# A hybrid decoder block on one core: one bank per token tile in the mixers, four weight slots in whole fp32, and one-hots on ScalarE

## The chip, the core and the metric

The kernel runs on one core of a Trainium2 chip. The metric is the device time of one execution in microseconds (us), and the median of several executions is what two kernels are compared by. The engines are called as the profile calls them: PE (TensorE matmul), PEld (its weight loads), DVE (VectorE), ACT (ScalarE), POOL (GpSimd) and SP (SyncE, which here only issues transfers).

## The reference, cut to what matters

512 tokens of width 1024 pass one layer: two token mixers beside each other, then a retrieval feed-forward in which every token picks 128 of 16,384 experts.

```python
h = rms_norm(x, norm1_g)
proj = h @ w_in
hq, hf, hi, hog, aq, ak, av, ga, gb = split(proj)
y_a = hgrn2_mixer(hq, hf, hi, hog, lb, hg_norm_g)          # gated recurrence, 4 heads
y_b = dilated_attention_mixer(aq, ak, av, q_norm_g, k_norm_g)
merged = sigmoid(ga) * (y_a @ w_branch_a) + sigmoid(gb) * (y_b @ w_branch_b)
x = x + merged @ w_out
h2 = rms_norm(x, norm2_g)
# PEER: 8 heads, top 16 of 128 keys twice, top 16 of the pairs: 128 experts a token
hid = einsum('thkd,td->thk', u[idx], h2)
a = gelu(hid) * gate
x = x + einsum('thk,thkd->td', a, v[idx])
```

All is float32. The kernel keeps that precision on PE in one of two ways: a whole fp32 product, which the profile shows as two records per matmul, or a split one, in which each operand is the sum of a high and a low half in fp32r and three products (high by high, high by low, low by high) are added.

## The kernel before, in words

Tokens come in four tiles of 128. The work has four stages, and I cut the trace by them.

- **First front**, 0 to 158 us: `Front((0,), split=False)` takes tile 0 through both mixers, the output product and the query product. Its products are whole fp32.
- **Second front**, 158 to 640 us: `Front((1, 2, 3), split=True)` does the same for the other three tiles with split products. `slot` loads weights, 256 columns of a matrix at a time (a slot), in units of four blocks of 128 rows (512 KB, two buffers `w`); `halves` makes `wh` on ACT (L98) and `wl` on DVE, or every fifth one on POOL (L99). `proj_T` puts 256 output columns on the partitions and streams 384 tokens; `proj_N` puts tokens on the partitions. `proj_N` kept two token tiles in one PSUM bank of the three called `pp`, and `products` held the second tile back until the slot's other products were done. Under this stage run `routing(0)` (top-16 searches on DVE, L536 to L615) and `u_steps(0)`: for tile 0 each expert's row of `u` is gathered by an indirect transfer of POOL (L638) and multiplied and summed with the token on DVE (L650), 128 rows.
- **Middle**, 640 to 1058 us: 72 blocks of `hidden` (tiles 1 and 2 against all experts, whole fp32, `ph<-h,ub`); `routing` of tiles 3, 1 and 2; and `scatter_steps`, 24 groups of 16 tokens, which turn gates and indices into a dense table. A group takes four one-hot pairs: `e1` (L689) and `e2` (L692) on DVE, `eg` which is `e2` times the weight, on ACT for `k` in `ACTW = (4, 12)` (L696) and on DVE otherwise (L698), then four matmuls into `pg` (L703, eight records), and ACT's copy to `Gx` (L704). `Gx` goes to DRAM as `g_d` (L706). Meanwhile 44 rows of `u` for tile 3 are gathered and summed (`u_steps(3)`, 0.6 of a row a block). A gather is tied to the `gelu` of the block just issued, which is `behind[0]`; its sum follows it in the program.
- **Final**, 1058 to 1781 us: 128 blocks of `acc` (split products with `v`, 18 matmuls), 56 more blocks of `hidden` with split products, the other rows of `u`, and 128 rows of `v` for tile 3. `Gc` is a group of eight blocks of the dense table, read back from `g_d` (L851, 1.5 MB), in two buffers by turns; DVE multiplies it by `pre` (L855) before `ah` and `al` are made of it.

Each engine runs its instructions in one fixed order, found when the kernel is built by a scheduler that estimates times; so the place of an instruction in its queue can differ from the place in the code.

Of the kernel before, what the change touches and what calls it, by code (L numbers as in the profile page):

```python
# [56 lines left out]
ACTW = (4, 12)  # L57
# [16 lines left out]
def kernel(ctx: ExitStack, tc: tile.TileContext, x, wst, par, cst, cols, g2, keys, u, v, ut, vr, out):  # L74
# [72 lines left out]
    class Front:  # L147


        def __init__(self, tiles, split, after_unit):  # L150
# [6 lines left out]
            lT = hp.tile([P, KC, NM], F32R, name="xl")[:, :, :N] if split else None  # L157
            g1 = par_sb[:, C_G1:C_G1 + KC]
            xs = hp.tile([P, NM // P, D], F32, name="pairB")
            for t in range(n):  # L160
# [5 lines left out]
                for c in range(0, KC, 4):  # L166
# [19 lines left out]
        def slot(self, i, ks):  # L186

            src = lambda k, n: wst[i][:, k * 256:(k + n) * 256].rearrange("p (k c) -> p k c", k=n)
            for k0 in range(ks.start, ks.stop, UK):
                n = min(UK, ks.stop - k0)  # L190
                if not self.split and k0 % (2 * UK):
# [7 lines left out]
                if not self.split:  # L199
                    yield k0 - ks.start, [w[:, k] for k in range(n)]  # L200
                    continue
# [6 lines left out]
        def products(self, i, ks, x, outs, w_stays):  # L208


            last = ks.stop - ks.start - 1
            units = []
            for k0, ws in self.slot(i, ks):
                units.append((k0, ws))
                for out, cut, alone in outs:
                    if alone:
                        accumulate(out, ws, x, cut, w_stays, k0, last)
            for out, cut, alone in outs:
                for k0, ws in units if not alone else ():
                    accumulate(out, ws, x, cut, w_stays, k0, last)  # L220

        def proj_T(self, i, x=None, ks=slice(0, KC)):

            outs = [psb.tile([P, 512], F32, name="pp")[:, :self.N] for _ in range(2)]
            self.products(i, ks, self.hT if x is None else x, [(pt, slice(j * P, (j + 1) * P), True) for j, pt in enumerate(outs)], True)
            return enumerate(outs)

        def proj_N(self, i, x=None):

            outs, parts = [], []  # L230
            for t0 in range(0, self.n, 2):
                m = min(2, self.n - t0)
                pt = psb.tile([P, 2, 256], F32, name="pp")[:, :m]
                parts += [(pt[:, t], slice((t0 + t) * P, (t0 + t + 1) * P), t == 0) for t in range(m)]
                outs.append((slice(t0, t0 + m), pt))
# [3 lines left out]
        def proj_hgrn(self):  # L239
# [4 lines left out]
            vs = hp.tile([P, 2, NM // P, 512], F32, name="vs")  # L244
            self.vt, self.sil = vs[:, 0], vs[:, 1]
# [26 lines left out]
            self.qd, self.ki, self.ksT = sq, G2, lf  # L272
            for b in range(2):
# [66 lines left out]
        def proj_attn(self):  # L340
# [3 lines left out]
            for b in range(3):  # L344
# [3 lines left out]
                for t in range(n if b else 0):  # L348
                    k0 = (T0 + t) * RQ
                    for r in range(NR):  # L350
                        nc.scalar.dma_start(out=vres[k0:k0 + RQ, b - 1, r], in_=vt[r::NR, t])
            for b in range(3):
# [3 lines left out]
                for ts, pt in self.proj_N(W_IN + 11 + b):  # L356
# [6 lines left out]
                for j in range(2):  # L363
                    pk2 = ps.tile([P, NM // P, P], F32, name="pt")
                    for t in range(n):
                        nc.tensor.transpose(pk2[:, t], kn[:, t, 2 * j:2 * j + 2].rearrange("p n e -> p (n e)"), ident)
                    nc.scalar.activation(kT[:, 2 * b + j, self.t0:self.t0 + N], pk2[:, :n].rearrange("p t q -> p (t q)"),
                                         AF.Copy, scale=kgain)
# [571 lines left out]
```

## Time and profile before

| | us |
|---|---|
| median of 3 executions (lowest, highest) | 1778.53 (1771.76, 1779.42) |
| the profiled execution, its own time | 1782.34 |
| its span, first to last instruction | 1780.6 |
| PE busy, DVE busy, ACT busy over the span | 1637.9, 1343.1, 702.0 |

How to read it: a busy PE is not PE at its best, since the ends of pipelined matmuls are modelled; the distance from one start to the next is the better price. The profile's share of time by engine is an average over four stages with different limits, so stretches are read one by one: in each, which wait of PE ends last, and which engine ended it. "granted clock" is the share of TensorE's full clock in a stretch.

### The profile page before, as it was taken

How to read it: one execution, taken by the hardware profiler on the slowest of the kernel's cores; microseconds unless marked ns; L12 is line 12 of the kernel's file. 1: busy time of each engine (PE TensorE's matmuls, PEld its weight loads, DVE VectorE, ACT ScalarE, POOL GpSimd, SP SyncE). 2: the span in 40 equal slices, each digit the busy share in tenths (PEclk: the TensorE clock that was granted, in tenths of full speed). 3: DMA queues.
4: the chain of work that ended last, by engine and by line, in shares of the span. 5: the costliest groups of instructions: out<-in, count | busy, mean ns of one | idle time of the engine just before them, and what ended most of it. 6: DMA issues, size and time to landing. Idle time of an engine off the chain costs nothing.

```text
span 1780.6 us, 26815 instructions
## 1 busy us (share of the span) xinstructions
PE 1637.9 (92%) x9725; PEld 1449.5 (81%) x9725; DVE 1343.1 (75%) x2805; ACT 702.0 (39%) x1283; POOL 663.1 (37%) x502
## 2 busy tenths in 40 slices
PE   8998969789978799899999979999999999999997
PEld 7887969679867798787888967788888878887886
DVE  3112999888888649997996567778788878888787
ACT  3323443324334544432454563333334333333332
POOL 0000256676552004344342114343344454454442
PEclk9999979989998899999999989999999999999999
DMA  8776368779885326565657769899999889998988
GB/s 289 233 231 229 105 229 280 261 250 327 304 313 203 126 100 217 207 210 189 232 200 247 246 214 332 314 327 333 342 344 337 305 308 340 342 326 318 332 296 297
DMA packets 173812, 473.41 MB, mean 266 GB/s; under 512 B 14832, under 2 KB 62192, under 8 KB 173680
## 3 DMA queue, kind: packets, MB, share of 16 engines
q1 hardware_dynamic: 116272, 268.47, 44.3%
q0 software_dynamic: 55296, 201.35, 31.9%
q10 hardware_dynamic: 2112, 1.88, 0.3%
q8 instruction: 77, 1.26, 0.3%
q14 instruction: 55, 0.45, 0.1%
HBM read 442.80 MB, written 27.79 MB: 264 GB/s over the span
## 4 chain that ended last, share of the span: by engine, by line
PE 39%; DVE 29%; DMA 23%; issue 5%; ACT 2%; POOL 2%; DVEq 0%; SPq 0%; POOLq 0%; ACTq 0%
PE pp L112 15%; PE acc L866 13%; DMA Gc<-g_d 7%; PE ph L112 7%; DMA w<-in_wst_dram 4%; DMA row<-in_u_dram,idx 2%; DVE e L689 2%; DVE h2g L669 2%; DVE rowx L650 2%; DMA rowx<-in_v_dram,idx 2%; DMA vb<-in_vr_dram 2%; DVE rq L650 2%; PE pg L703 1%; DVE wl L99 1%; DVE eg L698 1%
## 5 line engine op out<-in xcount | busy, mean ns | idle before, releaser
L112 PE MATMUL ph<-h,ub 128*128 128x256 f32 x1152 | 266.2, 387 | 0.0
L866 PE MATMUL acc<-vl,ah 128*128 128x512 f32 x768 | 241.2, 395 | 10.4 <-DVE vl L862 10.3
L112 PEld LDWEIGHTS ph<-h,ub 128*128 128x128 f32 x1152 | 219.3, 195 | 30.2 <-ACT eg L696 0.2
L866 PE MATMUL acc<-vh,al 128*128 128x512 f32 x768 | 239.9, 394 | 0.0
L866 PE MATMUL acc<-vh,ah 128*128 128x512 f32 x768 | 221.5, 392 | 3.6 <-ACT vh L860 3.6
L638 POOL DMA_INDIRECT rowx<-in_v_dram,idx x96 | 154.4, 1608 | 153.1 <-DVE h2g L669 62.4
L638 POOL DMA_INDIRECT rowx<-in_u_dram,idx x96 | 120.1, 1251 | 222.5 <-DVE rowx L650 65.4
L98 ACT ACTIVATE ah<-Gc 128x384 fp32r<-128x384 f32 x128 | 67.0, 524 | 318.9 <-PE acc L866 310.7
L866 PEld LDWEIGHTS acc<-vl,ah 128*128 128x128 f32 x768 | 143.2, 190 | 43.9 <-DVE vl L862 14.7
L866 PEld LDWEIGHTS acc<-vh,al 128*128 128x128 f32 x768 | 145.6, 190 | 31.7
L866 PEld LDWEIGHTS acc<-vh,ah 128*128 128x128 f32 x768 | 139.9, 188 | 29.7 <-ACT vh L860 4.0
L862 DVE TENSOR_TENSOR vl<-vb,vh 128x1024 fp32r<-128x1024 f32 x128 | 156.2, 1220 | 10.2 <-ACT vh L860 10.0
L860 ACT ACTIVATE vh<-vb 128x1024 fp32r<-128x1024 f32 x128 | 135.9, 1062 | 53.9 <-DMA vb<-in_vr_dram 50.9
L638 POOL DMA_INDIRECT rq<-in_u_dram,idx x96 | 119.8, 1248 | 92.1 <-DVE rq L650 57.6
L650 DVE SCALAR_TENSOR_TENSOR rowx<-rowx,h2g 128x1024 f32<-128x1024 f32 x96 | 121.2, 1267 | 33.2 <-DMA rowx<-in_u_dram,idx 33.0
L650 DVE SCALAR_TENSOR_TENSOR rq<-rq,h2g 128x1024 f32<-128x1024 f32 x96 | 132.5, 1383 | 16.3 <-DMA rq<-in_u_dram,idx 15.3
L98 ACT ACTIVATE wh<-w 128x512 fp32r<-128x512 f32 x144 | 88.7, 628 | 130.1 <-PE pp L112 65.1
L669 DVE SCALAR_TENSOR_TENSOR h2g<-rowx,hid,h2g 128x1024 f32<-128x1024 f32 x95 | 121.6, 1280 | 19.8 <-DMA rowx<-in_v_dram,idx 19.7
L112 PE MATMUL ph<-hH,ul 128*128 128x256 f32 x448 | 126.4, 282 | 5.4 <-DVE ul L99 5.4
L112 PE MATMUL ph<-hH,uh 128*128 128x256 f32 x448 | 126.0, 281 | 3.8 <-ACT pre L814 3.8
L703 PE MATMUL pg<-eg,e 128*128 128x128 f32 x768 | 105.3, 291 | 22.7 <-DVE eg L698 15.7
L112 PE MATMUL ph<-hL,uh 128*128 128x256 f32 x448 | 126.1, 281 | 0.0
(289 smaller groups left out, 3624.1 us busy)
## 6 DMA issues: line engine op xcount, KB each, us to landing
ub<-in_ut_dram SPq DMA_DIRECT2D x128, 512.0 KB
vb<-in_vr_dram SPq DMA_DIRECT2D x128, 512.0 KB
w<-in_wst_dram SPq DMA_DIRECT2D x107, 512.0 KB
g_d<-Gx SPq DMA_DIRECT2D x24, 960.0 KB
Gc<-g_d SPq DMA_DIRECT2D x15, 1536.0 KB
wh<-in_wst_dram SPq DMA_DIRECT2D x37, 256.0 KB
wl<-in_wst_dram SPq DMA_DIRECT2D x33, 256.0 KB
pairB<-in_x_dram SPq DMA_DIRECT2D x5, 512.0 KB
```

The source lines that it names most:

```text
L98: nc.scalar.activation(hi, x, AF.Copy)
L99: (eng or nc.vector).tensor_tensor(out=lo, in0=x, in1=hi.bitcast(F32), op=ALU.subtract)
L112: nc.tensor.matmul(out, l, r, start=(k == 0 and i == 0), stop=(k == last and i == len(ops) - 1))
L638: d = nc.gpsimd.indirect_dma_start(out=r, out_offset=None, in_=src, in_offset=bass.IndirectOffsetOnAxis(ap=index, axis=0))
L650: nc.vector.scalar_tensor_tensor(r, r, 1.0, h2g[T], op0=ALU.mult, op1=ALU.mult, accum_out=hid[:, g, j:j + 1])
L669: nc.vector.scalar_tensor_tensor(acc, r, hid[:, g, j:j + 1], acc, op0=ALU.mult, op1=ALU.add)
L689: nc.vector.tensor_tensor(out=e1, in0=iota[:, None, :, 0].to_broadcast(by_token), in1=pk[:, ti, 0, tk, None].to_broadcast(by_token), op=AL ...
L698: nc.vector.tensor_tensor(out=eg, in0=e2.rearrange("p k q -> p q k"), in1=pkw[:, ti, tk, None].to_broadcast(by_token), op=ALU.mult)
L703: nc.tensor.matmul(pt[:, q], e1[:, q0 + q], eg[:, q0 + q], start=True, stop=True)
L860: behind[:] = [nc.scalar.activation(vH, vb, AF.Copy)]
L862: nc.vector.tensor_tensor(out=vL, in0=vb, in1=vH.bitcast(F32), op=ALU.subtract)
L866: nc.tensor.matmul(acc[t][c], l.rearrange("p g t -> p (g t)")[:, t * P:(t + 1) * P], r[:, c * 512:(c + 1) * 512], start=(b == 0 and i == 0 ...
```

## The change

Seven edits.

1. In the second front the normalised input is also kept whole (`h32`, in the buffer `vs`), and the halves `hT` and `lT` are made from it afterwards, eight pairs of 128x384 in place of six of 128x512. The four slots of the recurrence's `q` and `f` (`W_IN` to `W_IN + 3`) multiply whole fp32 weights with `h32`; no `wh` and `wl` are made for them. The tile `vs` of `proj_hgrn` is therefore taken later.
2. `proj_N` uses one PSUM bank for each token tile, and nothing is held back.
3. The transposes of the normalised keys come one slot later (`turn_keys`).
4. In `routing` the chosen index is reduced straight into its destination; 16 casts and the copies of `idf` go.
5. A sum of `u` in the middle stage comes one row after its gather (`lag`), and is tied to the `gelu` that the next gather is tied to.
6. `ACTW` becomes a table by tile: all of `eg` for tiles 0 and 1 on ACT, for tile 2 as before.
7. `Gc` is asked for at block 1 of a group of eight, not at block 4.

```diff
-ACTW = (4, 12)
+ACTW = {0: (0, 4, 8, 12), 1: (0, 4, 8, 12), 2: (4, 12)}
...
+            self.h32 = hp.tile([P, KC, NM], F32, name="vs")[:, :, :N] if split else hT
...
-                        xg = sp.tile([P, 4, P], F32, name="pT")
-                        nc.vector.tensor_mul(xg, pt, gain)
-                        halves(hT[:, c:c + 4, tk], lT[:, c:c + 4, tk], xg)
+                        nc.vector.tensor_mul(self.h32[:, c:c + 4, tk], pt, gain)
...
+            for k in range(KC if split else 0):
+                halves(hT[:, k], lT[:, k], self.h32[:, k])
...
-            for k0, ws in self.slot(i, ks):
-                units.append((k0, ws))
-                for out, cut, alone in outs:
-                    if alone:
-                        accumulate(out, ws, x, cut, w_stays, k0, last)
-            for out, cut, alone in outs:
-                for k0, ws in units if not alone else ():
-                    accumulate(out, ws, x, cut, w_stays, k0, last)
+            for k0, ws in self.slot(i, ks, isinstance(x, tuple) or isinstance(x, list)):
+                for out, cut in outs:
+                    accumulate(out, ws, x, cut, w_stays, k0, ks.stop - ks.start - 1)
...
-            for t0 in range(0, self.n, 2):
-                m = min(2, self.n - t0)
-                pt = psb.tile([P, 2, 256], F32, name="pp")[:, :m]
+            for t in range(self.n):
+                pt = psb.tile([P, 2, 256], F32, name="pp")[:, :1]
...
-                for j, pt in self.proj_T(W_IN + b):
+                for j, pt in self.proj_T(W_IN + b, self.h32):
...
-                for j, pt in self.proj_T(W_IN + 2 + b):
+                for j, pt in self.proj_T(W_IN + 2 + b, self.h32):
...
             for b in range(3):
+                outs = self.proj_N(W_IN + 11 + b)
+                if b:
+                    turn_keys(b - 1, kn)
...
-                nc.vector.tensor_reduce(out=idf[:, n], in_=sel[:, :hc].rearrange("p c k -> p k c"), axis=AX.X, op=ALU.add)
-                if T in UG:
-                    hn = slice((b + n) * TOPK, (b + n + 1) * TOPK)
-                    nc.vector.tensor_copy(idx[:, UG.index(T), hn], idf[:, n])
+                    nc.vector.tensor_reduce(out=idx[:, UG.index(T), hn] if T in UG else full[:, hn],
...
+            asked.append(row(idx[:, g, j:j + 1], u))
+            if j < P - 1 and len(asked) <= lag[0]:
+                yield 1
+                continue
...
+                if lag[0] and behind:
+                    turn(d, "a sum's turn")
...
-                if k in ACTW:
+                if k in ACTW[T]:
...
-        if b % GB == GB // 2 and b + GB < NKEY:
+        if b % GB == 1 and b + GB < NKEY:
```

Where instructions now stand, at three places.

**PE, from the middle stage into the final one.** Names: `pg` is the matmul of a one-hot pair (four in a row), `ph` a block of `hidden` (`h,ub` whole, `hH`/`hL` split). Before, ten pairs stood with nothing between them behind the last whole block:

```order
L112 MATMUL ph<-hL,uh 128x256
L112 MATMUL ph<-hH,ul 128x256
L703 MATMUL pg<-eg,e_8746 128x128 x4
L703 MATMUL pg<-eg,e_8758 128x128 x4
L703 MATMUL pg<-eg,e_8805 128x128 x4
L703 MATMUL pg<-eg,e_8817 128x128 x4
L703 MATMUL pg<-eg,e_8832 128x128 x4
L703 MATMUL pg<-eg,e_8844 128x128 x4
L703 MATMUL pg<-eg,e_8894 128x128 x4
L703 MATMUL pg<-eg,e_8906 128x128 x4
L703 MATMUL pg<-eg,e_8921 128x128 x4
L703 MATMUL pg<-eg,e_8933 128x128 x4
```

Now pairs come two by two between eleven matmuls of whole blocks, and only four pairs are left behind the last of these (two of them shown):

```order
L719 MATMUL pg<-eg,e_8719 128x128 x4
L719 MATMUL pg<-eg,e_8731 128x128 x4
L112 MATMUL ph<-h_5853,ub 128x256 x11
L719 MATMUL pg<-eg,e_8746 128x128 x4
L719 MATMUL pg<-eg,e_8758 128x128 x4
L112 MATMUL ph<-h_5853,ub 128x256 x7
L112 MATMUL ph<-hH,uh 128x256
L112 MATMUL ph<-hL,uh 128x256
```

So some six of the ten pairs moved ahead of the last whole blocks.

**SP, the first read of the dense table.** `g_d` is the last write of the table, `vb` a block of `v`. Before, three blocks of `v` were asked for ahead of `Gc`:

```order
L706 DMA g_d<-Gx 128x1920 x2
L858 DMA vb<-in_vr_dram 128x1024 x3
L851 DMA Gc<-g_d 128x24x128
L806 DMA ub<-in_ut_dram 128x1024
L858 DMA vb<-in_vr_dram 128x1024 x2
```

Now one:

```order
L722 DMA g_d<-Gx 128x1920
L822 DMA ub<-in_ut_dram 128x1024
L876 DMA vb<-in_vr_dram 128x1024
L869 DMA Gc<-g_d 128x24x128
L876 DMA vb<-in_vr_dram 128x1024 x3
```

Two blocks of `v` moved behind that `Gc`. The other fourteen `Gc` stand behind 10, 18, 26 and so on to 114 blocks of `v` in both kernels.

**DVE, a `Gc` in the final stage.** The eight products with `pre` of the next group (`Gc<-pre,Gc`) stood amid this group's `al` and `vl`:

```order
L99 TENSOR_TENSOR al<-Gc,ah 128x384
L862 TENSOR_TENSOR vl<-vb,vh 128x1024
L855 TENSOR_TENSOR Gc<-pre,Gc 128x16x16 x8
L650 SCALAR_TENSOR_TENSOR row,hid<-row,h2g 128x1024
L99 TENSOR_TENSOR al<-Gc,ah 128x384
```

And now:

```order
L99 TENSOR_TENSOR al<-Gc,ah 128x384
L880 TENSOR_TENSOR vl<-vb,vh 128x1024
L873 TENSOR_TENSOR Gc<-pre,Gc 128x16x16 x8
L662 SCALAR_TENSOR_TENSOR rowx,hid<-rowx,h2g 128x1024
L99 TENSOR_TENSOR al<-Gc,ah 128x384
```

Nothing moved there but the names of the row buffers.

## Rows read from the trace of the kernel before

**Rows 1.** Windows by stage: us; PE, PEld, DVE, ACT, POOL busy; clock; DMA

```profile
158.00:640.00 482.00, 416.65 (x2911) 383.99 (x2910) 399.78 (x868) 194.72 (x397) 214.31 (x164) 0.91 0.68 233
640.00:1058.00 418.00, 386.39 (x2124) 344.39 (x2122) 336.85 (x1089) 193.49 (x396) 132.70 (x115) 0.96 0.61 208
1058.00:1781.00 723.00, 693.15 (x3624) 592.20 (x3624) 574.37 (x742) 266.65 (x368) 312.46 (x213) 0.99 0.92 324
```

**Rows 2.** Windows inside the middle stage, same columns

```profile
675.00:945.00 270.00, 247.61 (x1306) 217.05 (x1305) 252.28 (x880) 112.10 (x230) 114.02 (x94) 0.96 0.61 208
945.00:1033.00 88.00, 88.00 (x524) 80.67 (x524) 46.99 (x86) 47.42 (x99) 16.42 (x19) 1.00 0.71 243
1033.00:1068.00 35.00, 22.68 (x139) 20.82 (x138) 23.59 (x42) 22.36 (x40) 4.18 (x5) 0.85 0.62 229
```

**Rows 3.** Waits of PE, 640 to 1058: us, times, longest

```profile
PE pg L703 <- DVE eg L698: 15.7, 6, 5.4
PE pg L703 <- DVE e L689: 6.3, 6, 3.3
...
PE pg L703 <- ACT eg L696: 0.7, 2, 0.4
```

**Rows 4.** Groups of DVE and ACT, 640 to 1060: busy us, mean ns | idle before

```profile
L650 DVE SCALAR_TENSOR_TENSOR rowx<-rowx,h2g 128x1024 f32<-128x1024 f32 x33 | 44.7, 1354 | 27.7 <-DMA rowx<-in_u_dram,idx 27.6
L698 DVE TENSOR_TENSOR eg<-e,pkw 128x512 f32<-128x512 bf16 x47 | 38.5, 820 | 0.0
...
L704 ACT ACTIVATE Gx<-pg 128x512 f32<-128x512 f32 x96 | 95.3, 1064 | 72.9 <-PE pg L703 59.9 <-issue 13.0
L696 ACT ACTIVATE eg<-e,pkw 128x128 f32<-128x128 bf16 x188 | 60.4, 399 | 11.4 <-DVE pkw L628 6.4 <-DVE e L692 5.0
```

**Rows 5.** Timeline of PE, end of the middle stage: start, us, [idle before <-releaser]

```profile
1039.27 5.24 PE L703 MATMUL pg<-eg,e 128*128 128x128 f32 x24 [5.36 <-DVE eg L698]
```

**Rows 6.** Chain of waits, same stretch: start, us, what

```profile
1027.77 8.56 DMA rowx<-in_u_dram,idx
...
1058.05 4.74 DMA g_d<-Gx
...
1062.91 13.30 DMA Gc<-g_d
...
1080.66 4.62 PE acc L866 x12
```

**Rows 7.** Groups of DVE, 160 to 640, columns as in rows 4

```profile
L99 DVE TENSOR_TENSOR wl<-w,wh 128x512 fp32r<-128x512 f32 x120 | 85.1, 713 | 22.3 <-ACT wh L98 18.7 <-PE pp L112 3.3
...
L605 DVE CAST idx<-idf 128x16 int32<-128x16 f32 x8 | 5.8, 728 | 0.0
```

**Rows 8.** Table loads of ACT, 160 to 640

```profile
L144 ACT ACT_TABLE_LOAD x2 | 2.6, 1283 | 0.0
```

**Rows 9.** Timeline of PE in a split slot of 384 tokens

```profile
188.16 0.33 PE L112 MATMUL pp<-xl,wh 128*128 128x384 f32 x1
...
190.76 0.33 PE L112 MATMUL pp<-xl,wh 128*128 128x384 f32 x1
```

**Rows 10.** Chain of waits: whole fp32 blocks of 256; weight loads

```profile
62.83 5.73 DMA w<-in_wst_dram
...
311.56 10.13 DMA w<-in_wst_dram
...
953.09 4.75 PE ph L112 x22
```

**Rows 11.** Waits of PE, 158 to 640

```profile
PE pp L112 <- DVE wl L99: 12.6, 8, 3.9
...
PE pt L366 <- DVE s L361: 9.6, 2, 5.1
```

**Rows 12.** Waits of DVE for the table, final stage

```profile
DVE Gc L855 <- DMA Gc<-g_d: 69.0, 15, 7.2
```

**Rows 13.** Waits of PE, final stage

```profile
PE acc L866 <- DVE vl L862: 10.3, 9, 2.7
```

More of the change, by code (lines that the diff above doesn't have):

```diff
@@ L184, in rstd, with slot @@
             return st[:, 1:2]
-        def slot(self, i, ks):
+        def slot(self, i, ks, split):
             src = lambda k, n: wst[i][:, k * 256:(k + n) * 256].rearrange("p (k c) -> p k c", k=n)
@@ L190, in slot @@
                 n = min(UK, ks.stop - k0)
-                if not self.split and k0 % (2 * UK):
+                if not split and not self.split and k0 % (2 * UK):
                     for j in range(0, n, 2):
@@ L198, in slot @@
                 self.after_unit(nc.sync.dma_start(out=w[:, :n], in_=src(k0, n)))
-                if not self.split:
+                if not split:
                     yield k0 - ks.start, [w[:, k] for k in range(n)]
@@ L272, in proj_hgrn @@
             self.qd, self.ki, self.ksT = sq, G2, lf
+            vs = hp.tile([P, 2, NM // P, 512], F32, name="vs")
+            self.vt, self.sil = vs[:, 0], vs[:, 1]
             for b in range(2):
@@ L351, in proj_attn, with turn_keys @@
                         nc.scalar.dma_start(out=vres[k0:k0 + RQ, b - 1, r], in_=vt[r::NR, t])
+            def turn_keys(b, kn):
+                for j in range(2):
+                    pk2 = ps.tile([P, NM // P, P], F32, name="pt")
+                    for t in range(n):
+                        nc.tensor.transpose(pk2[:, t], kn[:, t, 2 * j:2 * j + 2].rearrange("p n e -> p (n e)"), ident)
+                    nc.scalar.activation(kT[:, 2 * b + j, self.t0:self.t0 + N], pk2[:, :n].rearrange("p t q -> p (t q)"),
+                                         AF.Copy, scale=kgain)
+            kn = None
             for b in range(3):
+                outs = self.proj_N(W_IN + 11 + b)
+                if b:
+                    turn_keys(b - 1, kn)
                 s2 = sp.tile([P, NM // P, 4, 64], F32, name="s2")
@@ L362, in proj_attn @@
                                             op=ALU.mult)
[L363 to L368, printed above, removed]
+            turn_keys(2, kn)
             qy = hp.tile([P, KC, NM], F32, name="vs")[:, :, :N]
@@ L601, in routing @@
                 nc.gpsimd.tensor_add(sel[:, :hc], sel[:, :hc], sel[:, hc:])
-                nc.vector.tensor_reduce(out=idf[:, n], in_=sel[:, :hc].rearrange("p c k -> p k c"), axis=AX.X, op=ALU.add)
-                if T in UG:
-                    hn = slice((b + n) * TOPK, (b + n + 1) * TOPK)
-                    nc.vector.tensor_copy(idx[:, UG.index(T), hn], idf[:, n])
-            hs = slice(b * TOPK, (b + 4) * TOPK)
-            idff = idf.rearrange("p h k -> p (h k)")
-            nc.vector.tensor_copy(full[:, hs], idff)
+                hn = slice((b + n) * TOPK, (b + n + 1) * TOPK)
+                with nc.allow_low_precision(reason="one of the summands is not zero"):
+                    nc.vector.tensor_reduce(out=idx[:, UG.index(T), hn] if T in UG else full[:, hn],
+                                            in_=sel[:, :hc].rearrange("p c k -> p k c"), axis=AX.X, op=ALU.add)
+            if T in UG and T in VD:
+                hs = slice(b * TOPK, (b + 4) * TOPK)
+                nc.vector.tensor_copy(full[:, hs], idx[:, UG.index(T), hs])
         gt = gate.rearrange("p (h k) -> p h k", k=TOPK)
@@ L640, in row @@
         if behind:
-            tc.add_manual_dep(d.ins, behind[0].ins.name, mybir.DependencyInfo(
-                mybir.DependencyClass.Sync, mybir.DependencyReason.DATA), reason="a row's turn")
+            turn(d, "a row's turn")
         return r
@@ L647, in u_steps @@
         g = UG.index(T)
+        asked = []
         for j in range(P):
-            r = row(idx[:, g, j:j + 1], u)
-            nc.vector.scalar_tensor_tensor(r, r, 1.0, h2g[T], op0=ALU.mult, op1=ALU.mult,
-                                           accum_out=hid[:, g, j:j + 1])
+            asked.append(row(idx[:, g, j:j + 1], u))
+            if j < P - 1 and len(asked) <= lag[0]:
+                yield 1
+                continue
+            while asked:
+                r = asked.pop(0)
+                jr = j - len(asked)
+                d = nc.vector.scalar_tensor_tensor(r, r, 1.0, h2g[T], op0=ALU.mult, op1=ALU.mult,
+                                                   accum_out=hid[:, g, jr:jr + 1])
+                if lag[0] and behind:
+                    turn(d, "a sum's turn")
+                if j < P - 1 and len(asked) <= lag[0]:
+                    break
             yield 1
@@ L838 @@
     rows.add(v_steps(3))
+    lag[0] = 0
     rctx.close()
```

19 lines of the change are left out of this document (9 added, 10 removed).

## The prediction, made before the changed kernel ran

> **What bounds the kernel now.** I read the windows by stage first, then the waits of PE in each stage, the groups of DVE and ACT, and last the chain of waits where a stage ends. In the second front DVE is busy 399.8 of 482 us and PE 416.7 [rows 1], and PE waits there for two things of DVE that the change touches: low halves of weights, 12.6 us, and the normalised keys before their transposes, 9.6 [rows 11]. The middle stage is three pieces [rows 2]. From 675 to 945 us DVE is the full engine: 252 of 270, PE 248. From 945 to 1033 PE is: 88.0 of 88.0, while DVE has 47. From 1033 to 1068 no engine is full; PE works 22.7 of 35 at a clock of 0.85, because ten one-hot pairs stand there with nothing between them, and the first has waited 5.36 us [rows 5] behind DVE, which was itself held 8.56 us by one gathered row of `u` [rows 6]. In all, PE waits 22.0 us for one-hots of DVE in this stage, and 0.7 for those of ACT [rows 3]. The final stage is PE's, 693 of 723 us [rows 1]; DVE's 69 us of waits for `Gc` [rows 12] reach PE as little more than the 10.3 us it waits for `vl` [rows 13]. So DVE work taken out counts up to 945 us, PE work counts everywhere, and DVE work in the final stage counts hardly at all.
>
> The sum is made against the profiled execution: span 1780.6, time 1782.3, which is 3.8 above the median of 1778.5.
>
> **Edit 1, four slots whole.** Sixteen blocks of weights need no halves. Thirteen of their `wl` were DVE's, 13 x 0.713 = 9.3 us [rows 7]; the 16 `wh` and three `wl` of ACT and POOL lie beside other work. On PE a split matmul of 384 columns costs 0.173 us, since 15 steps take 2.60 [rows 9]. The four slots have 4 x 8 blocks of rows x 2 column halves = 64 products; split, these are 192 matmuls, 33.3 us. Whole, they are 128 records. A whole record of 256 columns costs 4.75 / 22 = 0.216 [rows 10], so one of 384 columns 0.324, and 128 cost 41.4. PE gains 8.1 us of work and DVE loses 9.3.
>
> **Edits 2, 3 and 4 in the second front.** Eight casts of indices go, 8 x 0.728 = 5.8 us of DVE [rows 7]. One bank per tile means a few more small additions, chains and products, one for each of three tiles instead of one for two, some 3 us of DVE by my estimate from the size of these casts. ACT gets two more table loads, 2 x 1.28 [rows 8], beside other work. The keys a slot later put a slot of PE work into the 9.6 us of waiting [rows 11]. DVE's net saving is 9.3 + 5.8 - 3 = 12. If DVE sets the pace all 12 come out; if PE does, 8 are added. Since PE's waits that can go are 12.6 and 9.6, and PE was busier than DVE, neither end holds alone: I take **-4**, ends -12 and +8. The first front has its order unchanged: nothing.
>
> **Edit 6, one-hots on ACT.** Tile 1's groups, 32 `eg` of 512 columns, leave DVE at 0.82 each, 26 us [rows 4], and eight casts, at most another 6. ACT takes 128 pieces at 60.4 / 188 = 0.321, 41 us [rows 4], on 193 of 418 [rows 1], so it stays far from full. What is late next, from 675 to 945, is PE itself: its idle there is 22 us. Of the 22.0 us of named waits 5.4 lie in the tail [rows 3, 5]; the other 16.6 are what I count as gone: **-16**, ends 0 (ACT's pieces hold PE as DVE's did) and -33 (all the idle, and the 0.04 of clock missing over 270 us).
>
> **Edit 5, sums one row later.** DVE waits 27.7 us in the middle stage for rows of `u` [rows 4]. Between 945 and 1033 that costs nothing, since DVE is half empty; so the waits that vanish there are worth nothing. The new tie holds a sum until a `gelu` is done that the next gather also waits for. A gather waits on POOL's queue, a sum on DVE's, where one-hots stand behind it; but in the changed order PE has at least 6.6 us of matmuls (30 and more records of 0.216) between the block whose `gelu` is waited for and the next pair, at the last 4.6. The way that these cover is a `gelu`, about 1.1 by my estimate from a copy (1.06) of twice its size, the sum, 1.4, and two one-hots of 0.8 [rows 4], 4.1 in all. I cost it at nothing. If that cover were missing it would be about 1 us a row, 44 rows.
>
> **The tail.** Six of ten pairs now stand ahead of the last whole blocks. From 1033 to the end of the window are 35 us. The work in it is 80 records of `pg` (24 take 5.24 at the low clock [rows 5], so half of 0.218 each at the full one: 8.7 us) and 48 split matmuls of `hidden`, two thirds of 0.173 each: 5.5. So 14.2 of work and 21 of waiting and slow clock. Six tenths of the latter go: **-13**, ends 0 and -19.
>
> Behind the tail comes a cost. The chain goes from the last `g_d`, 4.74 us, over `Gc`, 13.30, to the products at 1080.66 [rows 6]. `Gc` of the second group stands ahead of two blocks of `v` on SP that it stood behind, and its products stand ahead of these blocks' `vl` on DVE, so DVE waits with them queued behind it. On PE only 24 split matmuls instead of 48 are left to lie beside that chain, 2.8 us less. The ends are 0, if the transfer lands earlier by what it was moved, and 5.5, if all that cover is gone. I take **+4.5**, near the upper, because the chain begins with the same write.
>
> **Edit 7, `Gc` earlier.** The other fourteen stand where they stood, on SP and on DVE, since a buffer is free only after the group before last. The 69 us [rows 12] stay: nothing.
>
> The sum is -4 - 16 - 13 + 4.5 = -28.5: 1782.3 - 28.5 = 1753.8, and 3.8 less for the median, **1750**. With each term's ends its own range is about 1736 to 1768.
>
> **The rivals.** *ACT holds PE (about the same time).* An `eg` of a group takes DVE 0.82 us and ACT four pieces, 4 x 0.321 = 1.28, 0.46 more, in a queue that also holds the copies `Gx` of 1.06 [rows 4]. If each of the 32 pairs pays the 0.46 and half a copy, that is 32 x (0.46 + 0.53) = 32 us: it eats the sum of -28.5, and gives about 1782. For it: PE follows the pairs closely. Against it: where ACT makes pieces now, PE waits 0.7 us in all [rows 3]. The Trainium skill's page "ScalarE: Activation LUTs" (Rules for kernel authors) says to put multiplications on VectorE and not on ScalarE; by that rule edit 6 alone would be a loss. The trace agrees on the price of one piece of work, 1.28 against 0.82, but it also shows DVE as the full engine there. Chance 0.17.
>
> *Whole weights arrive late (slower).* The scheduler's order puts whole slots closer to their weights: a unit of four blocks takes PE 16 records x 0.324 = 5.2 us, with two buffers. While gathers run, a load took 10.13 us [rows 10]. If the loads come one behind the other, each of the eight units waits for the difference, 4.9: that is 39 us at one place, the four slots; with the sum's other terms -28.5 + 39 it ends at about 1789, 1785 to 1795. It decides from a load of 5.2 + 28.5 / 8 = 8.8 us on: from there the kernel is slower than before. Against it: loads before the gathers took 5.73 [rows 10], and a split unit of 24 x 0.173 = 4.2 was fed. Chance 0.09.
>
> *DVE's saving counts whole.* If PE's waits of 22.2 us in the second front [rows 11] go as well as its 33 us in the middle, the sum is -12 - 33 - 13 + 4.5 = -53 or so: about 1725. For it: DVE's share of both stretches. Against it: PE would have to be full in each. Chance 0.14.
>
> *The table does come earlier.* If the `Gc` did land earlier, PE's idle of the final stage, 30 us by its windows [rows 1], would go in part: 10.3 [rows 13] to 30, with the sum about 1728. Against it: the places in the queues. Chance 0.04.
>
> **How the numbers follow.** The forecast has 0.56, the first rival 0.17, the second 0.09, the third 0.14, the last 0.04. Half a per cent is 9 us, about what a measurement of this kernel can tell. Faster by more than that: the forecast, the third and the last, 0.74; same, 0.17; slower, 0.09. The range leaves out the rivals on the upper side in most of their cases and takes in the third and the last: 1722 to 1776.
>
> **What would show it.** In the profile after, `pp<-vs,w` should have 128 records of 384 columns with 0.32 us from one start to the next; the second front some 478 us long; the middle about 390, with DVE near 305 busy in it, no waits of DVE for `rowx` of several us, PE's waits for `eg` a few us, about 320 pieces of `eg` on ACT, and no run of more than four pairs at its end. DVE should still wait about 69 us for `Gc`. I am wrong if PE waits for ACT's `eg` by more than 10 us (the first rival), if it waits for weights at the slots of `vs` (the second), or if the middle shrinks by less than 15 us with the waits for DVE gone, which would mean that they stood on another engine's work.

## The result: slower, and where the time went

The changed kernel takes 1790.35 us (median of 6 executions, 1786.51 to 1797.72) against 1778.97 for the kernel before: a ratio of 1.0067, with an interval of 1.0039 to 1.0094. I had forecast 1750. Put on the chip once more it stood at 1.0031 (1.0004 to 1.0058), so it is slower in both, by 0.3 to 0.7%.

I cut the profiled executions by what PE does: up to the first whole block of `hidden` (the fronts), from there to the first `acc` (the middle), and to the last `acc` (the final stage).

| us | fronts | middle | final |
|---|---|---|---|
| before | 658.6 | 408.8 | 705.3 |
| forecast of the change | -4 | -29 | +4.5 |
| changed | 674.9 (+16.3) | 394.0 (-14.8) | 709.9 (+4.6) |
| changed, another execution | 681.4 | 392.6 | 708.6 |

So the middle gained half of what I forecast, and the fronts lost more than that. From 158 us to the end of the fronts PE was idle for 65.4 us before and 75.4 now, and busy 6.3 us longer; edit 1 asked for 8.1 us more of its work.

The windows of the changed kernel by these stages, columns as in [rows 1]:

```profile
158.00:675.00 517.00, 441.64 (x2972) 391.78 (x2971) 401.25 (x884) 197.44 (x424) 210.59 (x161) 0.93 0.65 221
675.00:1069.00 394.00, 364.05 (x2031) 322.95 (x2032) 311.90 (x1036) 222.41 (x504) 139.05 (x116) 0.98 0.65 221
1069.00:1787.00 718.00, 689.86 (x3600) 590.86 (x3600) 571.02 (x732) 263.28 (x363) 317.31 (x212) 0.99 0.91 324
```

DVE's work did go down in the middle and ACT's went up, as intended (from the first whole block to the first `acc`, DVE was busy 338 us and is 312, ACT 191 and is 222). What PE waits for in the second front, which answers to [rows 11]:

```profile
PE pp L112 <- DVE s L367: 15.3, 2, 8.3
PE pt L349 <- DVE s L367: 8.2, 1, 8.2
PE pp L112 <- POOL wl L99: 7.6, 2, 6.6
PE pp L112 <- DVE wl L99: 6.5, 3, 3.1
PE pp L112 <- ACT wh L98: 4.9, 2, 2.5
PE pp L112 <- DVE vs L273: 4.8, 1, 4.8
...
PE pp L112 <- ACT vs L268: 1.7, 1, 1.7
```

The waits for DVE's low halves fell (12.6 became 6.5), but those for POOL's low halves and ACT's high ones grew (4.2 and 0.6 became 7.6 and 4.9), so that waits for halves of weights are 19.0 in all, after 17.4. The wait for normalised keys, `s` in the trace, was 9.6 and is now 23.5, and 15.3 of it has a new form: not a transpose waits for keys, but `pp`, the first product of the next slot. PE's timeline shows two of these waits:

```profile
364.43 0.28 PE L112 MATMUL pp<-wl,hT 128*128 128x256 f32 x1
371.73 0.55 PE L112 MATMUL pp<-wh,hT 128*128 128x256 f32 x1 [7.02 <-DVE s L367]
...
391.59 0.55 PE L112 MATMUL pp<-wh,hT 128*128 128x256 f32 x1 [8.32 <-DVE s L367]
```

Why `s` frees a product is seen on ACT and DVE at the same time. `L364` squares a key bank, `L365` is the sum of its squares, `L367` the product that reads the bank for the last time; `L662` is the sum of a row of `u`, and `L98` and `L99` make the halves of the next slot's weights. The first wait:

```profile
365.89 0.63 ACT L98 ACTIVATE wh<-w 128x512 fp32r<-128x512 f32 x1 [6.68 <-DMA w<-in_wst_dram]
366.43 0.64 ACT L364 ACTIVATE s<-pp 128x256 f32<-128x256 f32 x2
```

```profile
366.55 0.69 DVE L99 TENSOR_TENSOR wl<-w,wh 128x512 fp32r<-128x512 f32 x1
367.16 0.74 DVE L365 TENSOR_REDUCE rk<-s 128x4 f32<-128x256 f32 x2
367.82 1.22 DVE L662 SCALAR_TENSOR_TENSOR row<-row,h2g 128x1024 f32<-128x1024 f32 x1
368.96 0.08 DVE L662 DVE_READ_ACCUMULATOR row<-row,h2g 128x1 f32 x1
368.96 0.41 DVE L365 TENSOR_REDUCE rk<-s 128x4 f32<-128x256 f32 x1
369.29 0.23 DVE L145 RECIPROCAL rk<-rk 128x4 f32<-128x4 f32 x2
369.69 1.55 DVE L662 SCALAR_TENSOR_TENSOR rq<-rq,h2g 128x1024 f32<-128x1024 f32 x1 [0.17 <-DMA rq<-in_u_dram,idx]
371.17 0.08 DVE L662 DVE_READ_ACCUMULATOR rq<-rq,h2g 128x1 f32 x1
371.17 0.74 DVE L367 TENSOR_TENSOR s<-pp,rk 128x256 f32<-128x256 f32 x2
```

There are three banks named `pp`. A slot of three token tiles now holds all three, so the next slot can't start until DVE has read one. The slot ended at 364.7; the last read of a bank came at 371.2. Two queues held it. The squares stood on ACT behind a half whose weights landed only at 365.9; the next slot's first halves were ready at 366.5 and 367.2, so that PE would have waited some 2 of the 7.0 us in any case. Then two sums of `u`, 1.22 and 1.55 us, stood between the reads on DVE.

In the second wait the next slot's weights are there, and it is DVE's queue that holds the bank. From 383.3, the end of the slot, to 391.6 it holds three sums of `u` and 1.77 us of waiting for a gathered row, 5.4 of the 8.3 us:

```profile
384.59 1.21 DVE L662 SCALAR_TENSOR_TENSOR row<-row,h2g 128x1024 f32<-128x1024 f32 x1
...
386.66 1.21 DVE L662 SCALAR_TENSOR_TENSOR rq<-rq,h2g 128x1024 f32<-128x1024 f32 x1
...
389.87 1.23 DVE L662 SCALAR_TENSOR_TENSOR rq<-rq,h2g 128x1024 f32<-128x1024 f32 x1 [1.77 <-DMA rq<-in_u_dram,idx]
...
391.02 1.08 DVE L367 TENSOR_TENSOR s<-pp,rk 128x256 f32<-128x256 f32 x3
```

The key slots are not the only ones. `vs L273` in the list above is the product in which DVE reads the bank of an output gate (`hog`), and `vs L268` is ACT's copy of a bank of values (`hi`). PE waits 4.8 and 1.7 us for them, and in the kernel before it waits for neither. With them, PE's waits for held banks are 21.8 us.

The same stretch of time in the kernel before and in the changed one, where the granted clock is 0.91 and 0.81:

```profile
345.00:455.00 110.00, 95.44 (x643) 87.25 (x644) 97.51 (x175) 40.77 (x85) 76.56 (x58) 0.91 0.83 281
345.00:455.00 110.00, 80.83 (x485) 76.72 (x485) 87.50 (x164) 33.41 (x77) 67.10 (x54) 0.81 0.88 300
```

PE is now idle for 29.2 of these 110 us, where it was for 14.6.

In the middle, PE's waits (answering to [rows 3]) and DVE's:

```profile
PE pg L719 <- DVE e L705: 10.6, 12, 1.6
PE pr L625 <- DVE ssb L622: 5.9, 1, 5.9
...
PE pg L719 <- DVE eg L714: 2.8, 1, 2.8
...
PE pg L719 <- ACT eg L712: 1.8, 2, 1.2
```

```profile
DVE e L705 <- PE pg L719: 19.0, 15, 3.9
DVE e L708 <- ACT eg L712: 16.8, 19, 1.6
DVE rowx L662 <- DMA rowx<-in_u_dram,idx: 12.2, 7, 4.4
DVE row L662 <- DMA row<-in_u_dram,idx: 5.9, 3, 2.4
```

The wait for `eg` of DVE went from 15.7 to 2.8, but the one for `e`, the other one-hot, grew from 6.3 to 10.6. DVE waits less for rows (18.1, after 37.0), more for PE and for ACT (19.0 and 16.8, after 14.2 and 4.0), so that these waits together are about what they were.

### The profile page after: what moved, and what is told of

Read it like the earlier page. It is cut to its first block, busy times and chain, and to the rows that moved or that the text cites. A ratio compares the mean times of both kernels' runs of the same rounds, so it can differ in the third digit from the quotient of the medians.

```text
span 1787.1 us, 26798 instructions
## 1 busy us (share of the span) xinstructions
PE 1635.0 (91%) x9661; PEld 1432.3 (80%) x9661; DVE 1316.3 (74%) x2755; ACT 730.1 (41%) x1412; POOL 670.6 (38%) x499
## 4 chain that ended last, share of the span: by engine, by line
PE 35%; DVE 27%; DMA 23%; issue 8%; POOL 4%; ACT 2%; SPq 0%; DVEq 0%; POOLq 0%; ACTq 0%
PE acc L884 11%; PE pp L112 11%; PE ph L112 9%; DMA Gc<-g_d 9%; DMA rq<-in_u_dram,idx 4%; DMA w<-in_wst_dram 3%; DMA rowx<-in_v_dram,idx 2%; DVE rq L662 2%; DVE e L705 2%; DVE h2g L685 2%; PE pg L719 2%; DMA rowx<-in_u_dram,idx 2%; DVE vl L880 2%; DVE rowx L662 2%; DVE Gc L873 1%
## 5 line engine op out<-in xcount | busy, mean ns | idle before, releaser
L884 PE MATMUL acc<-vl,ah 128*128 128x512 f32 x768 | 240.0, 394 | 13.4 <-DVE vl L880 13.4
L643 POOL DMA_INDIRECT rowx<-in_u_dram,idx x96 | 132.5, 1380 | 216.0 <-DVE rowx L662 51.8
L643 POOL DMA_INDIRECT rowx<-in_v_dram,idx x96 | 147.2, 1534 | 173.8 <-DVE h2g L685 55.4
L98 ACT ACTIVATE ah<-Gc 128x384 fp32r<-128x384 f32 x128 | 67.0, 524 | 312.0 <-PE acc L884 306.5
L884 PEld LDWEIGHTS acc<-vl,ah 128*128 128x128 f32 x768 | 142.5, 189 | 45.7 <-DVE vl L880 16.8
L662 DVE SCALAR_TENSOR_TENSOR rq<-rq,h2g 128x1024 f32<-128x1024 f32 x96 | 133.0, 1388 | 29.8 <-DMA rq<-in_u_dram,idx 27.3
L98 ACT ACTIVATE wh<-w 128x512 fp32r<-128x512 f32 x128 | 78.8, 628 | 158.1 <-PE pp L112 90.7
L662 DVE SCALAR_TENSOR_TENSOR rowx<-rowx,h2g 128x1024 f32<-128x1024 f32 x96 | 118.9, 1239 | 27.8 <-DMA rowx<-in_u_dram,idx 24.3
L112 PE MATMUL pp<-wh,hT 128*128 128x256 f32 x376 | 111.0, 315 | 30.4 <-DVE s L367 15.3
```

Source lines behind the costliest of these rows:

```text
L98: nc.scalar.activation(hi, x, AF.Copy)
L112: nc.tensor.matmul(out, l, r, start=(k == 0 and i == 0), stop=(k == last and i == len(ops) - 1))
L643: d = nc.gpsimd.indirect_dma_start(out=r, out_offset=None, in_=src, in_offset=bass.IndirectOffsetOnAxis(ap=index, axis=0))
L662: d = nc.vector.scalar_tensor_tensor(r, r, 1.0, h2g[T], op0=ALU.mult, op1=ALU.mult, accum_out=hid[:, g, jr:jr + 1])
L884: nc.tensor.matmul(acc[t][c], l.rearrange("p g t -> p (g t)")[:, t * P:(t + 1) * P], r[:, c * 512:(c + 1) * 512], start=(b == 0 and i == 0 ...
```

## Experiments: the banks

Theory A: edit 2 leaves no free bank, and the reads that free one wait in DVE's queue. Rival B: the whole slots of edit 1 are the loss. Rival C: sums of `u` moved ahead of the keys in DVE's queue, whatever the banks.

**Edit 2 alone undone** (pairs of tiles in a bank, the second tile's products held back, as before):

```diff
-            for t in range(self.n):
-                pt = psb.tile([P, 2, 256], F32, name="pp")[:, :1]
+            for t0 in range(0, self.n, 2):
+                m = min(2, self.n - t0)
+                pt = psb.tile([P, 2, 256], F32, name="pp")[:, :m]
```

> The changed kernel with edit 2 alone undone: two token tiles share a PSUM bank again and the second one's products are held back; everything else as changed. Theory A (no free bank): with one bank per tile a slot of three tiles holds all three banks of pp, so the next slot's first product waits until DVE has read the first of them, and those reads stand behind row sums and gather waits in DVE's queue; PE's waits for s (15.3 + 8.2 us) should fall to about the 9.6 of before, the second front should be 13 to 22 us shorter than the changed kernel's 516.9 us, and the time about 1768 to 1776. Theory B (whole slots): the eight us of PE work of edit 1 are the loss, DVE's saving is swallowed by waits for gathers; then this edit changes nothing: 1786 to 1794, second front 512 to 520. Theory C (the order): sums of u moved ahead of the keys in DVE's queue because they start earlier; then PE still waits some 15 to 20 us for keys, and the time is 1782 to 1790.

Measured: 1776.13 us, ratio to before 0.9987 (0.9965 to 1.0009). Fronts 655.5, that is 19 us under the changed kernel. The waits for `s` are almost gone, and those for `vs L273` and `vs L268` with them; part of the time came back as waits for low halves (20.2, after 6.5), so that PE's idle time fell by 15.6:

```profile
PE pp L112 <- DVE wl L99: 20.2, 10, 5.7
...
PE pt L358 <- DVE s L376: 1.5, 1, 1.5
```

Theory A holds; by B nothing would have changed, and by C the waits would have stayed at 15 to 20 us. By the medians the gain is smaller than 19 us: 14 against the changed kernel's first ratio, 8 against its second.

**Four banks of `pp`**, taken from the transposes:

```diff
-    ps = fctx.enter_context(tc.tile_pool(name="ps", bufs=3, space=PSUM, side="right"))
-    psb = fctx.enter_context(tc.tile_pool(name="psb", bufs=3, space=PSUM, side="right"))
+    ps = fctx.enter_context(tc.tile_pool(name="ps", bufs=2, space=PSUM, side="right"))
+    psb = fctx.enter_context(tc.tile_pool(name="psb", bufs=4, space=PSUM, side="right"))
```

> The changed kernel whole, but PSUM is divided otherwise in the two fronts: four banks of pp and two of pt in place of three and three. Theory A: a slot of three tiles leaves one bank free, so PE starts the next slot at once; the waits of pp for s (15.3 us) go and the time falls by 10 to 20 us, to 1770 to 1780, less what two banks of pt cost. Theory B or C: no gain, 1786 to 1796.

Measured: 1779.91 us, 0.9997 (0.9964 to 1.003), fronts 668.8, waits of `pp` for `s` 4.5 instead of 15.3. The same division in the kernel before is its control:

> Control for the second experiment: the kernel before with four banks of pp and two of pt. If two banks of pt cost something by themselves, this is slower than before: ratio 1.002 to 1.008, and the second experiment understates what a free bank gives the changed kernel. If the fourth bank helps here too: 0.993 to 0.998.

It costs 0.8% there (1.008, 1.005 to 1.011; fronts 680.6). So the fourth bank gives the changed kernel a gain although the bank taken from the transposes costs the kernel before 0.8%.

**The slots split again:**

```diff
-                for j, pt in self.proj_T(W_IN + b, self.h32):
+                for j, pt in self.proj_T(W_IN + b):
...
-                for j, pt in self.proj_T(W_IN + 2 + b, self.h32):
+                for j, pt in self.proj_T(W_IN + 2 + b):
```

> The changed kernel with the four slots of edit 1 split again (the normalised input is still kept whole first and its halves made after). PE loses 8 us of work, DVE gets 13 wl (9.3 us) back. Theory A: the waits for banks stay (over 15 us), the time is 1783 to 1797. Theory B: the second front gets 8 to 15 us shorter, 1774 to 1782. Theory C: the start of the sums of u moves back, PE's waits for keys fall under 12 us, 1776 to 1786.

Measured: 1792.94 us, 1.0047 (1.0008 to 1.0086), fronts 678.3. PE still waits for the reads (9.1 for `rk` and 9.4 for `s`). B falls.

**Edit 2 alone on the kernel before** (the `proj_N` and `products` of the changed kernel, nothing else of it):

> The kernel before with edit 2 alone: one bank per token tile, nothing held back, keys turned at once as before. Theory A: slower than before by 12 to 25 us (1790 to 1804), with PE waiting for the reads of pp. Theory B or C: within 6 us of before (1773 to 1785).

Measured: 1797.55 us, 1.0097 (1.0069 to 1.0126), fronts 671.3 against 658.6. Here the keys are turned at once, and it is the transposes that wait for the same reads:

```profile
PE pt L357 <- DVE s L352: 20.9, 3, 10.7
```

So edit 2 costs 1% by itself; edit 3 moved two of the three waits from the transposes to the banks. Here too PE waits for a bank of values that ACT has yet to copy, 5.7 us.

**Reads with a high priority.** Meant to show whether the queue of sums is what holds the banks:

```diff
                 for ts, pt in outs:
-                    m = ts.stop - ts.start
+                    with tc.high_priority():
+                        m = ts.stop - ts.start
...
```

> The changed kernel with edit 2 kept, but the reads of the key banks (square, sum, root, product) are given a high priority when the order is made, so that they stand ahead of the sums of u in DVE's queue. If the queue is the larger part of the wait for a bank: PE's waits for s fall from 23.5 to under 12 us, the second front is 6 to 14 us shorter than the changed kernel's, ratio to before 0.998 to 1.003. If the chain of the reads itself is it: waits over 18 us, ratio 1.004 to 1.009.

Measured: 1.0046 (1.0016 to 1.0077), waits for `s` 15.9 and 7.6. But the order hardly moved: at one of the three slots the three reads now stand together, and ahead of the first read stand the same sums as before. It decides nothing. No experiment parts the queue of sums from the reads' own chain (square, sum, root, product); only the rows of the two waits above do. Read this one as a third execution of nearly the changed kernel, with the next one as the second.

> The changed kernel once more, for the spread of its stages in another execution: by theory A the second front is again 514 to 522 us, with PE's waits for s over 18 us, and the middle 393 to 397; the final stage may be anywhere from 695 to 712. Ratio 1.004 to 1.009.

Measured: 1.0031, stages in the table above; waits of 14.1 and 8.9, fronts a little longer than expected (523 us from 158 on, for 514 to 522), the ratio a little lower.

**Reads taken off DVE.** ACT copies each key bank, and the rest works on the copy; the number of banks is as in the changed kernel:

```diff
-                    nc.scalar.activation(s2[:, ts], heads(pt), AF.Square)
+                    nc.scalar.activation(kn[:, ts], heads(pt), AF.Copy)
+                    nc.scalar.activation(s2[:, ts], kn[:, ts], AF.Square)
...
-                    nc.vector.tensor_tensor(out=kn[:, ts], in0=heads(pt), in1=rk[:, 1, ts, :, None].to_broadcast([P, m, 4, 64]),
+                    nc.vector.tensor_tensor(out=kn[:, ts], in0=kn[:, ts], in1=rk[:, 1, ts, :, None].to_broadcast([P, m, 4, 64]),
```

> The changed kernel with edit 2 kept, but ACT copies each key bank to SBUF first and the square, the sum and the product work on the copy, so that a bank is free 0.4 us of ACT after its products and no longer waits for DVE. If the place of the reads in DVE's queue is what holds the bank: PE's waits of pp for s (14 to 16 us) vanish, those of the transposes for s may stay under 10, the second front is 10 to 18 us shorter than the changed kernel's 520 to 525, ratio to before 0.995 to 1.001. If three held banks cost in another way: waits go elsewhere, front over 516, ratio 1.003 to 1.007.

Measured: 1769.44 us, 0.9949 (0.9924 to 0.9974): 1% under the changed kernel, faster than before, and a little better than expected. Fronts 657.3. No wait for DVE's `s` is left among PE's, and in the same stretch as above PE is nearly full, at a granted clock of 0.97:

```profile
345.00:455.00 110.00, 101.70 (x739) 93.85 (x738) 95.68 (x188) 49.38 (x116) 66.08 (x54) 0.97 0.90 309
```

PE is busy 21 us longer in these 110 us. One bank per tile is no loss if the key banks are freed by an engine with room (ACT is busy 200 of the 499 us of this second front); PE still waits 5.5 us for ACT's copies of the value banks. The copy takes the reads out of DVE's queue and shortens the chain to them at once, so it does not tell the two apart. Its control is the same copy where pairs share a bank, on edits 5 and 6 alone:

> Edits 5 and 6 on the kernel before (0.9936 and 0.9945), with the key banks copied by ACT first as well. There PE waits 10 us for s at the transposes, not at the banks, so the copy should give little: second front 496 to 502, ratio 0.990 to 0.996. If it is under 0.990 the banks hold the kernel before as well.

Measured: 1.0002 (0.9981 to 1.0024), outside of what I expected: there the copy costs 0.6% against the same kernel without it (0.9936 and 0.9945, below), fronts 664.5. Why it costs that, I can't say; it shows that the copy's gain in the changed kernel is not a gain of copying as such.

## Experiments: the middle

**Edits 5 and 6 alone**, on the kernel before, twice; the core of it:

```diff
-ACTW = (4, 12)
+ACTW = {0: (0, 4, 8, 12), 1: (0, 4, 8, 12), 2: (4, 12)}
...
         rows.add(u_steps(3))
+        lag[0] = 1
```

> The kernel before with edits 5 and 6 alone (sums of u a row behind their gathers, all one-hots of tile 1 weighted on ACT). Theory M (the middle's gain is real but half of what was forecast): the middle stage from the first whole block to the first acc is 394 to 400 us instead of 408.8, the fronts are as before, and the time is 9 to 15 us under before (ratio 0.991 to 0.995). Rival N (given back): the final stage has its own pace, set by its transfers, and what the middle saves returns as waits there; ratio 0.997 to 1.002 with a middle under 400.

> Edits 5 and 6 alone, once more. If the 0.9936 was their effect: 0.991 to 0.996 again, and a middle of 397 to 401. If it was a fortunate draw, and these and edits 1, 3, 4 and 7 on top of them are alike: 0.996 to 0.999.

Measured: 0.9936 (0.9912 to 0.9959) and 0.9945 (0.9913 to 0.9977), middle 399.4 and 399.3. So the middle's gain is real, about 0.6%, and it is not given back later. (I wrote of tile 1 here and in the prediction; the 32 `eg` that go to ACT are those of tiles 0 and 1.)

**Edit 6 alone** (the first two of these lines):

> The kernel before with edit 6 alone (one-hots of tile 1 weighted on ACT, sums of u as before). If edit 6 carries the middle's saving: middle 394 to 400 us. If the moved pairs and the tail do, by edit 5: middle 404 to 410, ratio 0.997 to 1.002. If ACT holds PE (the first rival of the prediction): over 410, PE's waits for ACT's eg over 8 us.

Measured: 1785.95 us, 1.0037 (1.0005 to 1.0068): slower, middle 412.9. ACT is not what holds PE: no wait of PE for ACT's `eg` is among its seven largest. DVE's freed time went into waits for rows, 47.2 us where it was 37.0:

```profile
DVE rowx L650 <- DMA rowx<-in_u_dram,idx: 32.3, 16, 5.1
DVE e L689 <- PE pg L703: 19.4, 13, 4.4
DVE row L650 <- DMA row<-in_u_dram,idx: 14.9, 7, 4.6
```

**Edit 5 alone** (the last of them, with the new `u_steps`):

> The kernel before with edit 5 alone (a sum of u one row behind its gather). DVE's waits for rows of u in the middle stage fall from 37 us to under 20. If those waits count only in the tail: middle 400 to 407 us, ratio 0.995 to 1.000. If they count for nothing, middle 406 to 410. A middle under 400 would make it the main part.

Measured: 1.0008 (0.998 to 1.0036), middle 407.4. So the two edits are worth -9 to -10 us of middle together, +4 and -1 apart. With both, the waits for rows are small:

```profile
DVE row L661 <- DMA row<-in_u_dram,idx: 8.7, 4, 3.6
DVE rowx L661 <- DMA rowx<-in_u_dram,idx: 7.0, 6, 3.0
```

**More buffers for `e2`**, with edit 2 undone:

```diff
-                e2 = gb.tile([P, NKEY, GS], BF16, name="e2", bufs=2)
+                e2 = gb.tile([P, NKEY, GS], BF16, name="e2", bufs=4)
```

> The changed kernel with edit 2 undone, as in the first experiment, and four buffers instead of two for e2, the one-hot that ACT weights. In the changed kernel DVE waits 16.8 us in the middle for ACT to release an e2, 4.0 before. Theory M1: this is what ate the other half of edit 6's saving; the waits fall under 5, PE's waits for e (10.6) fall under 6, and the middle is 5 to 12 us shorter than the first experiment's 398.5. Rival: PE is full by then and only the name of the wait changes; middle 395 to 401. The time goes from about 1776 to 1766 to 1772, or stays.

Measured: 0.9967 (0.9936 to 0.9997), middle 396.4. DVE's wait for ACT did not fall (17.0), PE's for `e` did (7.2, after 9.7 in the first experiment, whose middle was 398.5). With twice the room DVE waits there all the same, and I have not shown why. My reading that this wait ate the other half of edit 6 falls; 2 us in one profile are no result.

## Experiments: what the other edits do

The first three are the kernel before with edits 5 and 6 and one more edit of the change's diff (1, 7, 4, in this order); the last is the changed kernel with edits 1 and 2 undone.

> The kernel before with edits 5 and 6 (ratio 0.9936 by themselves) and edit 1, the four whole slots. If DVE's 9 us less count: 0.990 to 0.993 and a second front under 498 us. If PE's 8 us more count: 0.996 to 1.000, second front 506 to 512. In between, they cancel.

> The kernel before with edits 5 and 6 and edit 7, the table asked for at block 1 of a group. By the prediction only the first read moves and delays the first products by 4.5 us: ratio 0.995 to 0.998 and the first two groups of blocks longer. If the place costs nothing: 0.992 to 0.995.

> The kernel before with edits 5 and 6 and edit 4, the index reduced straight into its place. Eight casts of 0.73 us go in the second front and eight small ones in the middle; DVE waits there for gathers anyway. If that hides them: 0.992 to 0.995. If DVE's time counts: 0.989 to 0.991. This is the version that should be the fastest.

> The changed kernel with edit 2 undone and the four slots split again, so edits 3 to 7 are left. If edit 1 is what cost the 0.5% between the first experiment (0.9987) and edits 5 and 6 alone (0.9936): 0.992 to 0.995. If edit 3, 4 or 7 did: 0.997 to 1.001.

| added to edits 5 and 6 | ratio to before | fronts | middle | final |
|---|---|---|---|---|
| nothing (twice) | 0.9936, 0.9945 | 658.3, 653.1 | 399.4, 399.3 | 710.0, 711.3 |
| edit 1, whole slots | 0.9988 (0.9962 to 1.0014) | 669.9 | 398.4 | 707.8 |
| edit 7, table at block 1 | 0.9965 (0.9938 to 0.9991) | 660.4 | 396.6 | 700.8 |
| edit 4, no casts | 0.9979 (0.9953 to 1.0004) | 656.7 | 394.3 | 697.2 |
| edits 3, 4, 7 | 0.9989 (0.9967 to 1.001) | 659.5 | 396.2 | 705.8 |
| edits 1, 3, 4, 7 (first experiment) | 0.9987 (0.9965 to 1.0009) | 655.5 | 398.5 | 699.3 |

None gains on edits 5 and 6 alone. Edit 1 looks like a loss of half a per cent in the first of these rows and like nothing between the last two; edit 4 has the shortest stages of all, but its profile was 16 us faster than its median. Three expectations came out as put and do not agree on where the loss lies: with edit 1 the second front is 511.9 us, inside the 506 to 512 for "PE's 8 us more count"; with edit 7 the ratio is inside the 0.995 to 0.998 for a delayed first read; and without edit 1 it is inside the 0.997 to 1.001 for a cost of edits 3, 4 or 7. Since every edit also reorders the queues elsewhere, I can't put a price on edits 1, 3, 4 and 7 one by one. That stays open. The casts were not the gain that I expected of them.

## Why the prediction was wrong

- **First front, nothing:** right; the same products end it, 0.9 us later.
- **Edit 1, PE +8.1, DVE -9.3:** the price of a whole record was right:

```profile
201.68 4.78 PE L112 MATMUL pp<-vs,w 128*128 128x384 f32 x14
```

  14 records in 4.78 us, the last one's tail included, are near the 0.324 that I used; from one start to the next are 0.32. At these slots no weights came late (PE waited 0.5 us for a load), so the slower rival did not happen.
- **Edit 2, the step that failed.** I priced it as a few more small additions, "some 3 us of DVE", and took -4 for the front; it was +16.3. I counted instructions and not who holds the banks: three banks, three tiles, none for the next slot. PE's waits for held banks, 21.8 us (some 2 of them would have gone to weights), stood in no term, and the term's upper end, +8, had no room for them. The name of the buffer and its number stood in the code; the reads of the key banks stood among sums of `u` in DVE's queue. Without edit 2 the fronts are 655.5, and with it, but the keys copied by ACT, 657.3, close to the 654.6 that I had forecast. So about 20 of the 40 us between forecast and result are this by the profiles; by the medians of these two versions, set against the changed kernel's two ratios, it is 8 to 14 and 15 to 21.
- **Edit 3:** I gave the keys a slot to hide in. That works as long as the next slot can start. Where pairs share a bank and keys are turned late, PE waits 1.5 us for `s`; at once, 9.6 [rows 11], and 9.0 and 10.6 (edits 5 and 6 alone, twice). Beside edit 2, two waits only changed their name and one stays, behind the last slot.
- **Edit 6, -16, a second step that failed, and edit 5, nothing.** Cut from the first whole block to the last, the kernel before and the changed one, columns as in [rows 1]:

```profile
658.60:1028.90 370.30, 347.91 (x1886) 308.29 (x1886) 313.08 (x1038) 166.16 (x340) 128.92 (x111) 0.97 0.63 214
674.90:1047.80 372.90, 350.80 (x1950) 310.31 (x1950) 300.65 (x1013) 213.30 (x489) 137.57 (x114) 0.99 0.64 218
```

  Six pairs more (some 5 us) lie in the second, so some 2 or 3 us were gained and not 16. I said that the 16.6 us of waits for `eg` and `e` would go. DVE lost work, but PE's idle time here is 22.1 us, as it was (22.4). In the whole middle the waits for both of DVE's one-hots went from 22.0 to 13.4, and the one for the gates' `ssb` grew from 3.0 to 5.9. My sign of being wrong, a middle shrunk by less than 15 us with DVE's waits gone, was met in its number (14.8), but the waits are not gone: PE still waits for `e`, which DVE makes, and DVE in turn for PE and ACT. What sets the pace of these pairs stays open. By themselves edit 6 lost and edit 5 was nothing; together they gave 9 to 10 us of the middle. So edit 5 is not a term of its own: it lets edit 6 count, since DVE otherwise spends the freed time waiting for the gather.
- **The rival that ACT holds PE:** PE waits 1.8 us for ACT's `eg`, not 10. The rule of the Trainium skill that I set beside it ("ScalarE: Activation LUTs", Rules for kernel authors: multiplications belong on VectorE) gives the right sign for edit 6 alone, 1.0037, and the wrong one with edit 5 beside it, 0.9936.
- **The tail, -13:** right in kind. From the last whole block to the first `acc` were 38.5 us, now 21.1; some 5 us of that are the six pairs that moved ahead of it, so 12 were gained. Only four pairs stand there, and PE waits 2.83 us ahead of the last two:

```profile
1049.55 1.95 PE L719 MATMUL pg<-eg,e 128*128 128x128 f32 x16
1055.62 3.62 PE L719 MATMUL pg<-eg,e 128*128 128x128 f32 x16 [2.83 <-DVE eg L714]
1068.89 1.39 PE L884 MATMUL acc<-vh,ah 128*128 128x512 f32 x3 [2.67 <-ACT vh L878]
```

- **The transition, +4.5, and edit 7:** the final stage is 4.6 longer, but that proves nothing. Over 20 profiles of all these kernels, its mean is 703.3 with the table at block 1 (ten of them) and 705.8 at block 4 (ten). DVE's wait for the table, 69.0 in [rows 12], is 75.5, so the other fourteen reads gave nothing that shows, as said.

```profile
DVE Gc L873 <- DMA Gc<-g_d: 75.5, 15, 7.8
```

- **The range:** the terms' ends as I gave them add up to -64 and +13.5, which is 1714 to 1792 and takes in the result. The sum's own range of 1736 to 1768 does not follow from them, and I said nowhere how I narrowed it.

Of the 40 us, then, 20 are the fronts and 14 the middle, by one profile of each kernel. The final stage came out as forecast, within a spread that proves nothing, and 5 us lie between the profiles and their medians (the one before stood 3.8 above its own, the one after 1.5 below). The two fastest versions are edits 5 and 6 alone and the changed kernel with ACT's copies, 0.5 to 0.6% under before; their intervals overlap.

## What to carry to other kernels

Before you give each tile a bank of its own, count the banks that are left when the next product starts, and look where the last read of a bank stands in the queue of its engine: what stands ahead of it there is the price. An engine with room can free the bank by a copy, and the same layout then gained here; where pairs shared a bank the copy lost 0.6%, so count first. And where two edits work on one engine's time, work out what it waits for next before you add their savings.

## What the runs showed that I had not expected

One profile is a poor witness for a stage. Its time can be 13 or 16 us from its kernel's median (the first experiment's and the one with edit 4 were the fastest of their ten and twelve executions). Over 20 profiles the final stage took between 694.7 and 713.1 us, though much the same products are in it; and the four profiles that were 10 to 16 us faster than their medians have the four shortest final stages, 694.7 to 699.3, so it is there that I would look for the difference. The two kernels profiled twice do not show it: their final stages agree within 1.3 us and their middles within 1.4, while their fronts lie 6.5 and 5.2 apart. So 20 us in the fronts can be read from one profile, and 5 us cannot.
